# Weights packed slot by slot, and their low parts made by a negative on ScalarE and an accumulating DMA

## The chip, the cores and the metric

The kernel runs on one core of a Trainium2 chip. The metric is the time of one execution on the device in microseconds (us); lower is better. The core has the engines TensorE (PE; its weight loads are shown apart as PEld), VectorE (DVE), ScalarE (ACT), GpSimd (POOL) and SyncE (SP, which issues transfers), and 16 DMA engines that all queues share.

## The reference

Two blocks run on 512 tokens of width 1024, all in float32. Block one has two layers; each normalizes, multiplies by `w_in`, forms five attention branches, and merges them through gates and `w_branch`:

```
h = _rmsnorm(x, norm_g)
p = _split_columns(h @ w_in)
... five branches y_a (dsa), y_b (fox), y_c (sb), y_d (nsa), y_e (mem) ...
merge = sigmoid(p['merge'])
merged = sum(merge * einsum('bsnc,ncd->bsnd', ys, w_branch), axis=2)
return x + merged @ w_out
```

Block two adds 256 context tokens. Its first part, called the conformer part here, is a projection with `ab_w_in`, a 31-tap convolution over time of 512 channels beside an mLSTM with four heads, and a projection with `ab_w_out`. An FFN (ffn0), an attention with low-rank projections (MLA) and a second FFN (ffn1) follow.

## The kernel before

Every large matrix is multiplied in split precision. A float32 weight W is split into hi = W rounded to the type fp32r and lo = W − hi; activations are split alike, and `mm3` makes each product out of three matmuls, hi·hi, hi·lo and lo·hi.

Weights come in **slots** of at most 128 partitions by 1024 elements (512 KB). A slot is `m` row tiles of 128 rows by `n` columns with m·n ≤ 1024, for instance eight row tiles by 128 columns of `w_in`. For a slot, `wtile` does three things:

- a DMA that SP issues fills `wraw` straight out of the matrix in DRAM; each partition gets m pieces of n elements (eight of 512 bytes for the slot just named);
- ACT copies `wraw` to `whi` (L119 `CAST whi<-wraw`, `nc.scalar.copy`), which rounds it;
- DVE or POOL computes `wlo` = `wraw` − `whi` (`tt`, L741 `TENSOR_TENSOR wlo<-wraw,whi`).

There are four buffers each of `wraw`, `whi` and `wlo`, so a slot can be prepared once the slot four before it has been used up. In all 461 slots pass.

Nothing runs in the order in which the code is written. The class `Plan` records every operation (which is why nearly all instructions have line L119, that of the recorder), and at each `flush` a list scheduler sorts a part's operations into an order for each engine, going by a table of durations. Operations recorded with `either` may go to one of several engines: `tt` to DVE or POOL, `ev` (evictions and copies) to DVE or ACT. Which one is the planner's choice, so a change of what an engine has to do also moves other work. Once the order is made it is fixed: an engine runs its instructions one after the other and waits where one isn't ready.

Three places in the program are spoken of later:

- **Block one, the merges** (`zm`): for each branch and each of eight column tiles d, a `w_in` slot gives 24 matmuls into `ps_mm`, ACT makes the gate (`ACTIVATE gt<-ps_mm`, a tanh), and six matmuls into `ps_br` use a `w_branch` slot, which is held for four values of d. Then comes `w_out`.
- **The conformer part:** DVE computes the convolution, 31 operations for each of four channel tiles (`SCALAR_TENSOR_TENSOR u<-apad,cw,u`, 128x783); beside it PE does the heads of the mLSTM, whose matrices `dm` DVE also multiplies. The `ab_w_out` slots (tile names `wlo`, `whi` like all) are prepared meanwhile.
- **The start:** `w_mem_kv` is loaded and split while the first normalizations run.

Of the kernel before, what the change touches and what calls it, by code (L numbers as in the profile page):

```python
# [19 lines left out]
P = 128  # L20
# [71 lines left out]


class Op:
    __slots__ = ("i", "prio", "alts", "left", "ready", "succ", "tiles", "first", "table", "nbytes", "best", "end", "vis", "done", "nm", "why", "cols", "preds", "port", "kind")


class PlannedPool:
# [34 lines left out]
class Plan:  # L133
# [55 lines left out]
    def cost(self, eng, name, outs, ins, a, k):  # L189
        n = max(self.size(x) for x in outs[:1] + [y for y in ins if name in ("tensor_reduce", "max")])  # L190
        if eng == "t":
            cols = self.size(outs[0])
            big = ins[0].dtype in (F32, F32R)
            if name == "transpose":
                return max(2 * cols / 2.4, 107.0) + 2.5 if big else 56.0
            if ins[0].dtype == F32:
                if outs[0].ap[0][1] == 32:
                    return cols / 2.4 + 8
                if outs[0].ap[0][1] == 64:
                    return max(2 * cols / 2.4, 107.0) + 11  # L200
                return 2 * max(2 * cols / 2.4, 107.0) + 5
            if ins[0].dtype == F32R:
                return max(cols / 2.255, 107.0) + 2.5
            return max(cols / 2.4, 53.0) + 2.5
        src_psum = any(self.in_psum(x) for x in ins)
        if eng == "s":
            c = n * 0.8333 + (51 if src_psum else 93)
            if len([x for x in ins if self.size(x) == 1]) and n > 1:
                c += 94
            return c + (92 if k.get("accum_out") is not None else 0)  # L210
        if eng == "v":
            if name == "memset":
                return n * 1.04 + 8
            if name == "reciprocal":
                return n * 8.33 + 65
            if name == "tensor_tensor_scan":
                return n * 2.08 + 65
            two = name in ("tensor_copy", "tensor_scalar", "scale") and not src_psum and not self.in_psum(outs[0])
            ptr = name in ("tensor_scalar", "scalar_tensor_tensor", "scale") and n > 1 and any(self.size(x) == 1 for x in ins)
            return n * (0.52 if two else 1.0417) + (129 if ptr else 67)  # L220
        if eng == "g":
            if name == "memset":
                return n * 0.9 + 30
            return n * (2.1 if name in ("tensor_tensor", "scale") else 4.2) + 150
        return 600.0
# [8 lines left out]
    def add(self, alts, name, a, k):  # L234
        outs = [a[0]]
        if k.get("accum_out") is not None:
            outs.append(k["accum_out"])
        ins = [x for x in a[1:] if _is_ap(x)] + [x for kk, x in k.items() if kk != "accum_out" and _is_ap(x)]
        op = Op()
        op.i = len(self.ops)  # L240
        op.prio = op.i
        op.alts = [(e, fn, self.cost(e, name, outs, ins, a, k)) for e, fn in alts]
        op.cols = 0.0
        if alts[0][0] == "t":
            dt = ins[0].dtype
            big = name != "transpose" and dt == F32
            op.cols = (4 if big else 1) * self.size(outs[0]) * ins[0].ap[0][1] / P
        op.port = self.shares(name, outs, ins)
        op.kind = None
        if alts[0][0] == "t":  # L250
            up = lambda x: 32 if x <= 32 else 64 if x <= 64 else 128
            op.kind = (name == "transpose", ins[0].dtype, up(ins[0].ap[0][1]), up(outs[0].ap[0][1]))
        op.left, op.ready, op.succ, op.done = 0, 0.0, [], False
        op.table = None
        if name == "activation":
            func = a[2] if len(a) > 2 else k.get("func")
            op.table = TABLES.get(str(func).split(".")[-1])
        op.nm, op.why = name + ":" + a[0].tensor.name.rsplit("_", 1)[0], None
        if name == "matmul" and ins[0].dtype == F32:
            op.nm += "*"  # L260
        op.nbytes = 4 * self.size(outs[0]) * outs[0].ap[0][1] if alts[0][0] == "y" else 0
        preds = set()
        tiles = []
        for ap, wr in [(x, False) for x in ins] + [(x, True) for x in outs]:
            nm = ap.tensor.name
            if nm in self.tile_of and nm not in tiles:
                tiles.append(nm)
            r = self.region(ap)
            W, R = self.hist.setdefault(nm, ([], []))
            hit = lambda q: q[0] < r[1] and r[0] < q[1] and q[2] < r[3] and r[2] < q[3]  # L270
            inside = lambda q: r[0] <= q[0] and q[1] <= r[1] and r[2] <= q[2] and q[3] <= r[3]
            mem = self.tile_of.get(nm)
            serial = wr and alts[0][0] == "t" and mem is not None and mem[2] == PSUM
            for q, o in W:
                if hit(q) or (serial and (o.alts if o.done else o.alts[0][0]) == "t"):
                    preds.add(o)
            if wr:
                for q, o in R:
                    if hit(q):
                        preds.add(o)  # L280
                W[:] = [(q, o) for q, o in W if not inside(q) or o is op]
                R[:] = [(q, o) for q, o in R if not inside(q)]
                W.append((r, op))
            else:
                R.append((r, op))
        if alts[0][0] == "t":
            tiles += [x.tensor.name for x in self.into if x.tensor.name not in tiles]
        preds.discard(op)
        op.preds = list(preds) if DEBUG else ()
        for p in preds:  # L290
            if p.done:
                at = p.end if len(op.alts) == 1 and p.alts == op.alts[0][0] != "y" else p.vis
                op.ready = max(op.ready, at)
            else:
                p.succ.append(op)
                op.left += 1
        op.tiles = tiles
        self.ops.append(op)
# [86 lines left out]
    def flush(self):  # L385
# [97 lines left out]
        while remaining:  # L483
# [114 lines left out]
                GAPS[kk] = GAPS.get(kk, 0) + t - free[e]  # L598
            free[e] = end
            vis = end + self.LAT[e]  # L600
            if e == "y":
                dma_free = max(t + 1300, dma_free) + o.nbytes / 350.0
                vis = dma_free + 300
            o.end, o.vis = end, vis
            order.append((t, len(order), fn))
            if DEBUG:
# [31 lines left out]
                        parked[tag] = []  # L638
            for q in o.succ:
                q.left -= 1  # L640
                at = end + self.SAME[e] if len(q.alts) == 1 and q.alts[0][0] == e and e != "y" else vis
                if q.alts[0][0] == "t" and e != "t":
                    at += self.TO_PE
                if at > q.ready:
                    q.ready, q.why = at, o.nm
                if q.left == 0:
                    push(q)
# [46 lines left out]
class Net:  # L694
    def __init__(self, ctx, tc, I):
        ctx.enter_context(tc.manual_schedule())
        self.plan = self.nc = Plan(tc)
        self.tc, self.I, self.ctx = tc, I, ctx
        self.ahead = {}
        self.cst = self.plan.pool(ctx, "cst")  # L700
        self.wp = self.plan.pool(ctx, "wp")
        self.mm = self.plan.pool(ctx, "mm", PSUM)
        self.dr = ctx.enter_context(tc.tile_pool(name="dr", bufs=1, space=bass.MemoryType.DRAM))
# [60 lines left out]
    def wraw(self, src, m, n):  # L764
# [2 lines left out]
        self.nc.sync.dma_start(rv, src.rearrange("(k p) n -> p k n", p=P))  # L767
        return rv

    def prefetch(self, src, n, count, keep=True):  # L770

        K = src.shape[0]
# [10 lines left out]

    @staticmethod
    def key(src, m, n):
        return src.tensor.name, src.offset, m, n

    def wtile(self, src, m, n):
        if self.key(src, m, n) in self.ahead:
            return self.ahead.pop(self.key(src, m, n))  # L790
        rv = self.wraw(src, m, n)
        hi = self.wp.tile([P, 1024], F32R, tag="whi", name="whi", bufs=4)
        lo = self.wp.tile([P, 1024], F32R, tag="wlo", name="wlo", bufs=4)
        hv = hi[:, :m * n].rearrange("p (k n) -> p k n", n=n)
        lv = lo[:, :m * n].rearrange("p (k n) -> p k n", n=n)
        self.nc.scalar.copy(hv, rv)
        self.tt(lv, rv, hv.bitcast(F32), ALU.subtract, m * n)
        return hv, lv

    def mm3(self, ps, a, b, start, stop):  # L800
# [940 lines left out]
class BlockTwo:  # L1741
# [485 lines left out]
    def ffn(self, l, h, xT, xc, beside=None, after=None):  # L2227
# [5 lines left out]
        with ExitStack() as c2:  # L2233
            wk = n.plan.pool(c2, f"ffn{l}")
            n.wk, n.nt2 = wk, 6
            first = len(n.plan.ops)
            w = I["ffn_w_in_2"][l]
            starts = [1, S + 2]
# [252 lines left out]
def body(tc, I, out):  # L2491
    with ExitStack() as ctx:
        net = Net(ctx, tc, I)
        nc = net.nc
        net.consts(net_off())
        xp = net.plan.pool(ctx, "xp")
# [5 lines left out]
        for d in range(KD):  # L2502
            nc.sync.dma_start(out[d * P:(d + 1) * P, :], xT[:, d])
        net.plan.flush()


def net_off():
    return const_arrays()[1]


_INS = ["positions", "norm_g", "w_in", "kv_norm", "w_uk", "w_uv", "fox_bias", "nsa_pe_k", "nsa_pe_v",
        "nsa_wc1_k", "nsa_wc2_k", "nsa_wc1_v", "nsa_wc2_v", "mem_norm", "w_mem_kv", "w_branch", "w_out", "final_norm",
# [29 lines left out]
```

## Time and profile before

| | |
|---|---|
| time, median of 3 runs (us) | 3224.23 (3220.99 to 3225.24) |
| the profiled execution (us) | 3226.99, its span 3224.5 |
| mean granted TensorE clock in it | 0.975 of full speed |
| PE busy | 94% |
| DVE busy | 71% |
| ACT busy | 43% |
| POOL busy | 6% |
| moved by DMA | 287.9 MB, 89 GB/s over the span |

The profile is of one execution; busy time of an engine leaves out waits and the issuing of DMAs. In the rows further down PE's share is that of matmuls whose ends are modelled, so that idle time between matmuls is read better than the duration of one. In time, block one takes about 0 to 1500 us, the conformer part 1500 to 1890, ffn0 to 2440, MLA to 2860, and ffn1 the rest.

### The profile page before, as it was taken

Reading aid. Unit: us, or ns where it says so; the run is one execution under the profiler, and the core shown is the slowest. Engines: PE = TensorE matmul, PEld = TensorE weight load, DVE = VectorE, ACT = ScalarE, POOL = GpSimd, SP = SyncE. Lnnn points to the kernel's source line nnn. Section 1 sums busy time; section 2 is a strip of 40 time slices with the busy share of each in tenths; the row PEclk is TensorE's granted clock in tenths of the full one; section 3 lists DMA queues with packets and bytes.
Section 4 is the critical chain, followed back from the end, with each engine's and each line's share of the span. In section 5 each row is a group of like instructions: output and inputs, shape, how many; then the busy total and the mean of one; then the engine's idle time right before and its main releaser. Section 6 shows DMA issues by size and latency. Waiting matters only on the chain.

```text
span 3224.5 us, 43815 instructions
## 1 busy us (share of the span) xinstructions
PE 3042.2 (94%) x16384; PEld 2506.6 (78%) x16392; DVE 2300.3 (71%) x4600; ACT 1379.4 (43%) x2840; POOL 202.4 (6%) x197
## 2 busy tenths in 40 slices
PE   6899898999899898998997999999999999989999
PEld 5678776787778687787976888888887777768887
DVE  8795878756896778756899677655547878765555
ACT  5544545424445445424325632222225766642332
POOL 1100000001100000001222010000000001110000
PEclk9899999999999899999998999999999999999999
DMA  6343142444342142443310124334322100023323
GB/s 172 94 111 97 46 128 76 118 128 126 104 115 80 49 127 69 121 124 102 101 59 27 47 79 125 106 109 139 106 60 74 30 10 28 27 76 108 105 78 93
DMA packets 383597, 287.90 MB, mean 89 GB/s; under 512 B 13324, under 2 KB 352536, under 8 KB 383128
## 3 DMA queue, kind: packets, MB, share of 16 engines
q1 hardware_dynamic: 383384, 285.10, 30.6%
q8 instruction: 129, 2.11, 0.3%
q14 instruction: 84, 0.69, 0.1%
HBM read 269.72 MB, written 8.52 MB: 86 GB/s over the span
## 4 chain that ended last, share of the span: by engine, by line
PE 47%; DVE 11%; ACT 3%; DMA 3%; issue 2%; SPq 0%; POOL 0%; DVEq 0%; ACTq 0%; POOLq 0%
PE ps_mm L119 39%; DVE u L119 3%; DMA wraw<-in_ada_wT_dram 2%; PE ps_tp L119 2%; PE ps_pv L119 2%; PE ps_lg L119 2%; PE ps_br L119 1%; PE ps_nd L119 1%; DVE mx L119 1%; ACT p L119 1%; DVE y_mod L119 1%; DVE wlo L741 1%; PE ps_st L119 1%; DVE ada_junk L119 1%; DVE sq L119 0%
## 5 line engine op out<-in xcount | busy, mean ns | idle before, releaser
L119 ACT CAST whi<-wraw 128x1024 fp32r<-128x1024 f32 (+8 forms) x461 | 409.3, 889 | 817.9 <-PE ps_mm L119 749.7
L119 PE MATMUL ps_mm<-h_ffn,whi 128*128 128x512 f32 (+1 forms) x2112 | 565.0, 356 | 7.4 <-ACT h_ffn L119 5.5
L741 DVE TENSOR_TENSOR wlo<-wraw,whi 128x1024 fp32r<-128x1024 f32 (+5 forms) x389 | 402.0, 1034 | 134.3 <-ACT whi L119 129.6
L119 PEld LDWEIGHTS ps_mm<-h_ffn,whi 128*128 128x128 f32 x2112 | 375.5, 190 | 68.2 <-ACT h_ffn L119 7.9
L119 PE MATMUL ps_mm<-hh,whi 128*128 128x512 f32 x960 | 389.5, 406 | 3.4 <-ACT whi L119 3.4
L119 PE MATMUL ps_mm<-hl,whi 128*128 128x512 f32 x960 | 388.9, 405 | 0.0
L119 PE MATMUL ps_mm<-hh,wlo 128*128 128x512 f32 x960 | 387.7, 404 | 0.0
L119 PE MATMUL ps_mm<-h_ffn,wlo 128*128 128x512 f32 (+1 forms) x1056 | 374.3, 355 | 0.0
L119 DVE CUSTOM_DVE_ANT_0 ada_junk<-wraw,cond,cols 128x1024 bf16<-128x1024 f32 x160 | 209.2, 1308 | 107.5 <-DMA wraw<-in_ada_wT_dram 106.2
L741 POOL TENSOR_TENSOR wlo<-wraw,whi 128x1024 fp32r<-128x1024 f32 (+4 forms) x72 | 152.9, 2128 | 1389.5 <-ACT whi L119 811.5
L119 PEld LDWEIGHTS ps_mm<-h_ffn,wlo 128*128 128x128 f32 x1056 | 200.1, 190 | 27.6
L119 PEld LDWEIGHTS ps_mm<-hh,whi 128*128 128x128 f32 x960 | 182.8, 190 | 38.3 <-ACT whi L119 4.6
L119 PEld LDWEIGHTS ps_mm<-hh,wlo 128*128 128x128 f32 x960 | 182.5, 190 | 35.1 <-DVE wlo L741 1.0
L119 ACT ACTIVATE p<-ps_lg,mx 128x384 f32<-128x384 f32 (+3 forms) x288 | 155.8, 544 | 122.9 <-DVE mx L119 119.0
L119 PEld LDWEIGHTS ps_mm<-hl,whi 128*128 128x128 f32 x960 | 182.8, 190 | 33.0
L119 PE MATMUL ps_mm<-fhi,whi 128*128 128x512 f32 (+1 forms) x528 | 187.6, 356 | 2.6 <-DVE xT L119 2.6
L119 PE MATMUL ps_mm<-flo,whi 128*128 128x512 f32 (+1 forms) x528 | 188.3, 357 | 0.0
L119 PE MATMUL ps_mm<-fhi,wlo 128*128 128x512 f32 (+1 forms) x528 | 187.6, 355 | 0.0
L119 DVE SCALAR_TENSOR_TENSOR xT<-ps_mm,mod,xT 128x512 f32<-128x512 f32 x136 | 101.7, 749 | 88.5 <-PE ps_mm L119 88.0
L119 DVE TENSOR_REDUCE mx<-ps_lg 128x1 f32<-128x384 f32 (+3 forms) x288 | 143.8, 505 | 25.9 <-PE ps_lg L119 22.5
L119 PE MATMUL ps_tp<-ident,p 128*128 128x128 f32 x768 | 131.9, 282 | 18.2 <-DVE p L736 8.3
L119 PEld LDWEIGHTS ps_tp<-ident,p 128*128 128x128 f32 x768 | 91.4, 142 | 62.7 <-ACT p L737 20.1
(533 smaller groups left out, 6314.6 us busy)
## 6 DMA issues: line engine op xcount, KB each, us to landing
wraw<-in_w_in_dram SPq DMA_DIRECT2D x132, 512.0 KB
wraw<-in_ada_wT_dram SPq DMA_DIRECT2D x96, 512.0 KB
wraw<-in_ffn_w_in_dram SPq DMA_DIRECT2D x88, 512.0 KB
wraw<-in_ffn_w_out_dram SPq DMA_DIRECT2D x64, 256.0 KB
wraw<-in_w_branch_dram SPq DMA_DIRECT2D x20, 512.0 KB
wraw<-in_w_out_dram SPq DMA_DIRECT2D x16, 512.0 KB
wraw<-in_ab_w_in_dram SPq DMA_DIRECT2D x16, 512.0 KB
wraw<-in_ffn_w_out_dram SPq DMA_DIRECT2D x32, 192.0 KB
```

What stands on the lines that cost most here:

```text
L119: return plan.add([(eng, lambda: fn(*a, **k))], name, a, k)
L741: f = lambda x: x.tensor_tensor(out, a, b, op=op)
```

## The change

Two things change.

**Packing.** The host lays out all slots, in the order in which the program asks for them, in one array `in_w_dram` of 461 x 128 x 1024 elements. A slot is then one block in which each partition's elements lie together (4 KB for a full slot), and SP loads it with one DMA as before.

**Low parts.** While `lo_by_dma` is set, which is through block one and the conformer part, `wlo` is not a subtraction any more. ACT writes the negated and rounded weights into `wlo` (`activation`, Copy with scale −1), and a DMA issued by POOL reads the slot from DRAM a second time and adds it to `wlo` (`accum_op=ALU.add`). The first call of `ffn` clears the flag; from there on DVE or POOL subtracts as before. 230 slots are made in the new way: 187 subtractions leave DVE and 43 leave POOL, 230 activations come to ACT, and 230 DMAs to POOL's queue. The number of SP's DMAs doesn't change. The planner gets a cost for a DMA on POOL and its landing, and moves some 60 evictions from ACT to DVE (`pT`, `yh`, `sb_v`, `p` and others).

```diff
@@ cost
         if eng == "g":
+            if name == "dma_start":
+                return 1000.0
@@ flush
-            if e == "y":
+            if o.dma:
                 dma_free = max(t + 1300, dma_free) + o.nbytes / 350.0
-                vis = dma_free + 300
+                vis = dma_free + (300 if e == "y" else 1500)
@@ class Net
+    lo_by_dma = True
+
+    def packed(self, src, m, n):
+
+        self.packs.append((src, m, n))
+        return self.I["w"][len(self.packs) - 1][:, :m * n]
+
+    def wpacked(self, src, m, n):
+        raw = self.wp.tile([P, 1024], F32, tag="wraw", name="wraw", bufs=4)
+        dr = self.packed(src, m, n)
+        self.nc.sync.dma_start(raw[:, :m * n], dr)
+        return raw[:, :m * n].rearrange("p (k n) -> p k n", n=n), dr
...
     def wtile(self, src, m, n):
...
-        rv = self.wraw(src, m, n)
+        rv, dr = self.wpacked(src, m, n)
...
         self.nc.scalar.copy(hv, rv)
-        self.tt(lv, rv, hv.bitcast(F32), ALU.subtract, m * n)
+        if self.lo_by_dma:
+
+            self.nc.scalar.activation(lv, rv, AF.Copy, scale=-1.0)
+            self.nc.gpsimd.dma_start(lo[:, :m * n], dr, accum_op=ALU.add)
+        else:
+            self.tt(lv, rv, hv.bitcast(F32), ALU.subtract, m * n)
         return hv, lv
@@ ffn
             n.wk, n.nt2 = wk, 6
+            n.lo_by_dma = False
@@ kernel
+    for slot, (src, m, n) in zip(w, packs, strict=True):
+        slot[:, :m * n] = src.reshape(m, P, n).transpose(1, 0, 2).reshape(P, m * n)
```

What it does to the order on the engines is seen at three places. The first is ACT in the merge of the last branch (dsa) of layer 0, before; `gt` is the gate, `mh` the merged result that goes on to `w_out`:

```order
L119 ACTIVATE gt<-ps_mm 128x512
L119 CAST whi<-wraw 128x1024
L119 ACTIVATE gt<-ps_mm 128x512
L119 CAST whi<-wraw 128x1024 x2
L119 ACTIVATE gt<-ps_mm 128x512
L119 CAST whi<-wraw 128x1024
L119 ACTIVATE gt<-ps_mm 128x512
```

And now, on the same engine at the same place:

```order
L119 CAST whi<-wraw 128x1024
L119 ACTIVATE gt<-ps_mm 128x512
L119 ACTIVATE wlo<-wraw 128x1024
L119 CAST whi<-wraw 128x1024
L119 ACTIVATE gt<-ps_mm 128x512
L119 ACTIVATE wlo<-wraw 128x1024
L119 CAST whi<-wraw 128x1024
L119 ACTIVATE wlo<-wraw 128x1024
L119 CAST whi<-wraw 128x1024
L119 ACTIVATE gt<-ps_mm 128x512
```

A slot's negative stands behind its cast and, mostly, behind a gate that waits for PE. The second place is POOL in the conformer part; `b` and `M` are matrices of the mLSTM, `u<-u,mu` the layer norm behind the convolution, `gpad` the first instruction of ffn0. Before:

```order
L741 TENSOR_TENSOR wlo<-wraw,whi 128x1024
L119 MEMSET apad 128x15 x6
L741 TENSOR_TENSOR wlo<-wraw,whi 128x1024 x4
L119 MEMSET b 64x768
L119 MEMSET M 64x768
L741 TENSOR_TENSOR wlo<-wraw,whi 128x1024 x12
L741 TENSOR_TENSOR u<-u,mu 128x512 x4
L741 TENSOR_TENSOR u<-u,mu 128x256 x3
L119 MEMSET gpad 128x1 x9
```

And now:

```order
L119 DMA wlo<-in_w_dram 128x792 x2
L119 DMA wlo<-in_w_dram 128x528
L119 DMA wlo<-in_w_dram 128x1024 x2
L119 MEMSET b 64x768
L119 DMA wlo<-in_w_dram 128x1024 x2
L119 MEMSET M 64x768
L119 DMA wlo<-in_w_dram 128x1024 x12
L744 TENSOR_TENSOR u<-u,mu 128x512 x4
L119 DMA wlo<-in_w_dram 128x1024 x8
L119 MEMSET gpad 128x1 x9
```

POOL has no subtraction left there, and the last eight slots of `ab_w_out`, which were DVE's, now stand on POOL behind the layer norm. The third place is DVE at the last channel tile of the convolution, whose taps stand between the products `dm` of the heads. Before:

```order
L119 TENSOR_SCALAR u<-apad,cw,cols 128x783
L119 SCALAR_TENSOR_TENSOR u<-apad,cw,u 128x783 x20
L119 TENSOR_TENSOR dm<-ps_mb,u 128x128
L119 SCALAR_TENSOR_TENSOR u<-apad,cw,u 128x783
L119 TENSOR_TENSOR dm<-ps_mb,u 128x128
```

And now:

```order
L119 TENSOR_SCALAR u<-apad,cw,cols 128x783
L119 SCALAR_TENSOR_TENSOR u<-apad,cw,u 128x783 x31
L728 COPY mv<-ps_mm 128x4x128
L119 SCALAR_TENSOR_TENSOR u<-apad,cw,u 128x783
L119 TENSOR_TENSOR dm<-ps_mb,u 128x128
L119 SCALAR_TENSOR_TENSOR u<-apad,cw,u 128x783
L119 TENSOR_TENSOR dm<-ps_mb,u 128x128
```

More of the taps now stand ahead of the first `dm`.

## Rows read from the trace of the kernel before

**Rows 1.** The page's first part: busy time, share of the span, instructions.

```profile
span 3224.5 us, 43815 instructions
PE 3042.2 (94%) x16384; PEld 2506.6 (78%) x16392; DVE 2300.3 (71%) x4600; ACT 1379.4 (43%) x2840; POOL 202.4 (6%) x197
```

**Rows 2.** Busy time by stretch: PE, PEld, DVE, ACT, POOL; clock; DMA share; GB/s.

```profile
0.00:1500.00 1500.00, 1384.33 (x7146) 1126.92 (x7155) 1131.99 (x2422) 692.22 (x1343) 84.94 (x76) 0.97 0.37 105
1640.00:1760.00 120.00, 100.83 (x513) 82.54 (x511) 110.69 (x165) 38.99 (x108) 32.69 (x15) 0.89 0.15 44
```

**Rows 3.** Chain that ended last, 1590 to 1840 us: start, us, what.

```profile
1647.59 31.06 DVE u L119 x27
1682.34 20.45 DVE u L119 x22
```

**Rows 4.** Six stretches of block one, sums; all work, then the subtractions.

```profile
sum 220.00, PE 195.04 PEld 157.79 DVE 208.64 ACT 127.23 POOL 23.33; mean PE 32.51 PEld 26.30 DVE 34.77 ACT 21.21 POOL 3.89
...
sum 220.00, PE 77.02 PEld 41.40 DVE 14.34 POOL 17.84; mean PE 12.84 PEld 6.90 DVE 2.39 POOL 2.97
```

**Rows 5.** Waits of PE, 0 to 1890 us: total, times, longest; then of PEld.

```profile
PE ps_z L119 <- DVE sb_later L741: 11.8, 9, 2.4
...
PEld ps_mm L119 <- DVE wlo L741: 1.0, 2, 0.8
```

**Rows 6.** Lines by form, 0 to 1890 us: busy, mean ns | idle before, releasers.

```profile
L119 ACT CAST whi<-wraw 128x1024 fp32r<-128x1024 f32 x204 | 213.7, 1049 | 351.7 <-PE ps_mm L119 295.0 <-issue 38.8 <-DMA wraw<-in_w_in_dram 8.1
L741 DVE TENSOR_TENSOR wlo<-wraw,whi 128x1024 fp32r<-128x1024 f32 x168 | 205.0, 1221 | 117.5 <-ACT whi L119 116.7
...
L119 DVE SCALAR_TENSOR_TENSOR u<-apad,cw,u 128x783 f32<-128x783 f32 x120 | 138.1, 1188 | 0.6
...
L741 POOL TENSOR_TENSOR wlo<-wraw,whi 128x1024 fp32r<-128x1024 f32 x36 | 100.4, 2794 | 651.3 <-ACT whi L119 651.3
```

**Rows 7.** The subtractions alone by stretch: PE, PEld, DVE, POOL, clock, DMA share, GB/s.

```profile
0.00:1500.00 1500.00, 636.66 (x1690) 326.35 (x1691) 206.81 (x173) 62.67 (x26) 0.97 0.37 105
1640.00:1760.00 120.00, 34.97 (x95) 18.17 (x94) 0.00 (x0) 25.84 (x8) 0.89 0.15 44
```

**Rows 8.** Timeline of POOL and DVE, 1696 to 1722 us: start, us, instruction.

```profile
1701.94 12.23 POOL L741 TENSOR_TENSOR wlo<-wraw,whi 128x1024 fp32r<-128x1024 f32 x4 [34.59 <-ACT whi L119]
...
1702.90 2.97 DVE L119 SCALAR_TENSOR_TENSOR u<-apad,cw,u 128x783 f32<-128x783 f32 x1
...
1715.12 1.02 DVE L119 SCALAR_TENSOR_TENSOR u<-apad,cw,u 128x783 f32<-128x783 f32 x1
```

**Rows 9.** The taps: durations in ns, min/median/max, first and last start.

```profile
L119 DVE SCALAR_TENSOR_TENSOR u<-apad,cw,u x120: 1018/1026/3171, 1557.4 to 1733.1; 128x783 f32<-128x783 f32 x120
```

**Rows 10.** Timeline of ACT in a merge, 1400 to 1445 us: start, us, instruction, idle before.

```profile
1414.53 1.05 ACT L119 CAST whi<-wraw 128x1024 fp32r<-128x1024 f32 x1 [5.42 <-PE ps_mm L119]
1415.49 0.58 ACT L119 ACTIVATE gt<-ps_mm 128x512 f32<-128x512 f32 x1
```

**Rows 11.** Chain in ffn0, 1990 to 2300 us: DMAs from issue to landing.

```profile
2072.09 3.46 DMA wraw<-in_ada_wT_dram
...
2077.61 5.02 DMA wraw<-in_ada_wT_dram
```

**Rows 12.** Chain in that merge, 1384 to 1440 us: start, us, what.

```profile
1414.73 1.37 PE ps_br L119 x6
1416.10 5.59 PE ps_mm L119 x24
...
1430.04 5.59 PE ps_mm L119 x24
```

**Rows 13.** Two short stretches, columns as in group 2.

```profile
640.00:720.00 80.00, 80.00 (x352) 64.63 (x353) 49.85 (x71) 23.55 (x32) 0.00 (x0) 1.00 0.45 129
20.00:30.00 10.00, 2.60 (x9) 1.59 (x9) 7.41 (x14) 8.83 (x17) 0.00 (x0) 1.00 1.02 285
```

**Rows 14.** GB/s at the start, 0 to 30 us in slices of 0.75.

```profile
GB/s 0 0 90 88 322 153 350 415 295 235 376 412 358 411 415 381 124 4 6 100 276 337 320 294 267 320 357 345 342 306 296 290 292 290 309 333 198 315 347 19
```

More of the change, by code (lines that the diff above doesn't have):

```diff
@@ L94 @@
 class Op:
-    __slots__ = ("i", "prio", "alts", "left", "ready", "succ", "tiles", "first", "table", "nbytes", "best", "end", "vis", "done", "nm", "why", "cols", "preds", "port", "kind")
+    __slots__ = ("i", "prio", "alts", "left", "ready", "succ", "tiles", "first", "table", "nbytes", "best", "end", "vis", "done", "nm", "why", "cols", "preds", "port", "kind", "dma")
 class PlannedPool:
@@ L260, in add @@
             op.nm += "*"
-        op.nbytes = 4 * self.size(outs[0]) * outs[0].ap[0][1] if alts[0][0] == "y" else 0
+        op.dma = name == "dma_start"
+        op.nbytes = 4 * self.size(outs[0]) * outs[0].ap[0][1] if op.dma else 0
         preds = set()
@@ L291, in add @@
             if p.done:
-                at = p.end if len(op.alts) == 1 and p.alts == op.alts[0][0] != "y" else p.vis
+                at = p.end if len(op.alts) == 1 and p.alts == op.alts[0][0] and not p.dma else p.vis
                 op.ready = max(op.ready, at)
@@ L640, in flush @@
                 q.left -= 1
-                at = end + self.SAME[e] if len(q.alts) == 1 and q.alts[0][0] == e and e != "y" else vis
+                at = end + self.SAME[e] if len(q.alts) == 1 and q.alts[0][0] == e and not o.dma else vis
                 if q.alts[0][0] == "t" and e != "t":
@@ L698, in __init__ @@
         self.tc, self.I, self.ctx = tc, I, ctx
-        self.ahead = {}
+        self.ahead, self.packs = {}, []
         self.cst = self.plan.pool(ctx, "cst")
@@ L785, in key @@
     def key(src, m, n):
-        return src.tensor.name, src.offset, m, n
+        return src.__array_interface__["data"][0], m, n
     def wtile(self, src, m, n):
@@ L2493, in body @@
         net = Net(ctx, tc, I)
+        packs = net.packs
         nc = net.nc
@@ L2504, in body @@
         net.plan.flush()
+    return packs
 def net_off():
     return const_arrays()[1]
+_STREAMED = ("w_in", "w_mem_kv", "w_branch", "w_out", "ab_w_in_2", "ab_w_out_2", "mla_w_in_2", "mla_w_uq_2", "mla_w_ukv_2",
+             "mla_w_out_2", "ffn_w_in_2", "ffn_w_out_2")
+SLOTS = 461
 _INS = ["positions", "norm_g", "w_in", "kv_norm", "w_uk", "w_uv", "fox_bias", "nsa_pe_k", "nsa_pe_v",
@@ L2532 @@
             name, a = "ada_wT_2", np.ascontiguousarray(a.transpose(0, 2, 1))
-        put(name, a)
+        if name in _STREAMED:
+            I[name] = a
+        else:
+            put(name, a)
     for name, src in (("xT", "x"), ("memT", "mem"), ("ctxT", "ctx_2")):
@@ L2536 @@
     put("consts", const_arrays()[0])
+    I["w"] = nc.dram_tensor("in_w_dram", (SLOTS, P, 1024), F32, kind="ExternalInput").ap()
     out = nc.dram_tensor("out_0_dram", (D, S), F32, kind="ExternalOutput").ap()
     with tile.TileContext(nc) as tc:
-        body(tc, I, out)
+        packs = body(tc, I, out)
+    w = np.zeros((SLOTS, P, 1024), np.float32)
+    for slot, (src, m, n) in zip(w, packs, strict=True):
+        slot[:, :m * n] = src.reshape(m, P, n).transpose(1, 0, 2).reshape(P, m * n)
+    arrays["in_w_dram"] = w
     r = bass_utils.run_bass_kernel_spmd(nc, [arrays], core_ids=[0])
```

## The prediction

> **What bounds the kernel now.** I read the page's totals first, then busy time by stretch, the groups of instructions by form, the waits of PE, the chain of work that ended last, and timelines of single stretches. PE is busy for 3042 of 3224.5 us and DVE for 71% [rows 1]: TensorE is the bound nearly everywhere, and no matmul is taken away here. Something is to be had only where PE stands idle or runs at a lower clock, and where DVE is what it waits for. Block one leaves PE idle for 1500 − 1384.3 = 115.7 us; in the middle of the conformer part PE is busy for 100.8 of 120 us at a clock of 0.89 while DVE is busy for 110.7 [rows 2]. There the chain runs through the convolution's taps, 31.1 and 20.5 us at a stretch [rows 3]. In block one DVE sets the pace in short pieces: in six stretches of 220 us together, which I chose because DVE is nearly full in them (208.6 us), PE is idle for 25.0 us [rows 4]; a typical single wait there is that for `sb_later`, 11.8 us in nine pieces [rows 5]. For low parts themselves PE waits almost never: 1.0 us for those of DVE in all of this [rows 5].
>
> **What is removed.** A subtraction of a full slot takes 1.221 us on DVE and 2.794 on POOL [rows 6]. Of those of DVE 168 are full ones, 205 us, nearly all in block one, where DVE spends 206.8 us on all its subtractions and POOL 62.7 [rows 7].
>
> The conformer part first. POOL makes eight low parts between 1640 and 1760 us, 25.8 us, and DVE none [rows 7]; still DVE is slowed by them. Four of them in a row on POOL take 12.2 us from 1701.9 on, and the taps that start meanwhile take 2.97 us; as soon as POOL is done a tap takes 1.02 [rows 8]. The median of the 120 taps is 1.026 us, their mean 1.188, so that 120 x 0.162 = 19.4 us of DVE go to such meetings [rows 6, 9]. With a DMA on POOL in place of the subtraction they should end. How much of it reaches the end of the part? At least these four taps' delay, 4 x (2.97 − 1.02) = 7.8. At most all of PE's loss in that stretch, 19.2 us idle and 0.11 x 100.8 = 11.1 of clock [rows 2]: 30. The taps lead the chain for most of the stretch, so I take nearly the whole relief: **−18 us** (−30 to −7.8). What is late next are the heads' own products and `ab_w_out`, whose slots now queue on POOL behind the layer norm; that queue was idle for hundreds of us before its subtractions [rows 6], and I give it nothing.
>
> In block one the relief of DVE is larger, some 200 us, and the share that lies on the path smaller. In the six stretches the subtractions cost DVE 14.3 us, and POOL's 17.8 us beside them hold up what DVE does then, if it acts as in the conformer part [rows 4]. The idle time of PE there, 25.0 us, is the most to be had; the least is nothing, since about 60 evictions come from ACT to DVE and the planner can spend the gap on them. I take less than DVE's own 14.3: **−10 us** (−25 to 0).
>
> **What is added.** *ACT.* 230 negatives of the size of the cast, 1.049 us for a full slot [rows 6]: at most 241 us, fewer for small slots. ACT is busy for 692 of 1500 us in block one [rows 2]; with nearly all of these it comes to about 930, or 62%, less what it passes to DVE. In the six stretches it is at 127 of 220. It is covered by PE's matmuls, since ACT waits for PE for 295 us ahead of casts alone [rows 6]; in the sum 0. Without that cover a negative costs PE 1.05 us each time.
>
> *The way to a low part.* Before: cast, then 1.2 us of DVE. Now: cast (1.05), mostly a gate (0.58, [rows 10]), the negative (1.05), POOL's issue, and a DMA that has to land. An accumulating DMA is nowhere in the trace. An ordinary load of 512 KB takes 3.46 to 5.02 us from issue to landing where the chain waits for it [rows 11]; below I take that, above twice the longer one, 10 us. So the way is 6.1 to 12.7 us. What is there for it: in a merge a d takes 5.59 + 1.37 = 6.96 us [rows 12], and a slot cast at 1414.5 is used at 1430.0, a lead of 15.5 us [rows 10, 12]. That is enough at either end. It is not where two `w_branch` slots are held at once, of four buffers, so that the `w_in` slots rotate through two: the lead is then about 6.96 + 1.37 = 8.3 us. There are 2 layers x 5 branches x 2 = 20 such places. At the lower end nothing is late; at 10 us of landing 4.4 us are, of which a change of the order by the planner saves some: I set the upper bound at 2 us a place, +40. I choose a landing near that of the ordinary load, since as much data is read, and add a little for the places where it is longer: **+3 us** (0 to +40). Only POOL's other work queues behind a DMA that waits there, and that is 84.9 us in block one, most of it subtractions [rows 2, 7].
>
> [...]
>
> *The DMA engines.* They move 105 GB/s in block one at a share of 0.37 [rows 2]. The load is densest between 640 and 720 us, 129 GB/s at 0.45 [rows 13], that is 10.3 MB, about 20 slots. At the start 512 KB go at up to 415 GB/s where pieces are long (`xT`, 4 KB a row) and near 300 where they are 512 bytes (the slices from the 24th on) [rows 14]: 1.3 against 1.7 us. Packed, 20 loads take 26 us of these 80; 14 accumulating DMAs (DVE made 14 low parts there) take 18 us if they go like a load, 37 if at half its rate. It is full only if one costs more than three loads, 26 + 55 = 81. In the sum 0.
>
> *Packing* itself shortens a load by 0.4 us, but casts wait for raw data for only 8.1 us in 1890 [rows 6]: 0. Where the new low parts aren't used the order of work is nearly as before: 0.
>
> *The start.* From 20 to 30 us the DMA engines are full (1.02), PE does 2.6 us [rows 13], and `w_mem_kv` is being loaded; each of its low parts now needs a second DMA. For the first four slots I count 4 x 1.3 = 5 us more against 4 x 0.4 less: **+4 us** (0 to +12).
>
> **Sum.** −18 − 10 + 3 + 4 = −21 against the 3227.0 us of the profiled execution, whose 2.5 us outside the span [rows 1] don't change: 3206. That execution lies 2.8 us above the median of 3224.2, so for the median I say **3203 us**, 0.7% faster. About 0.2%, 6.4 us, is what a measurement of this kernel can tell from no change.
>
> **Rivals.** *Low parts land late* (slower). If an accumulating DMA lands after more than 8.3 − 2.7 = 5.6 us, all 20 places wait; at two us each the sum is −18 − 10 + 40 + 4 = +16, 3240, and with the 4.4 us of the upper end each, +88, nearer to 3290. For it: the chain of five steps through three queues and half the slots' lead. Against it: everywhere else there are 15.5 us. It decides for slower from some 31 us of waits on, 1.5 us a place.
>
> *ACT takes DVE's place* (no change). ACT sits in the path of the gates and of `p`; if its negatives, which can stand ahead of an eviction, cost PE as much as DVE gives back, a tenth of the 230 on the path is 24 us: 3224. For it, ACT at 58% in the six stretches already; against it, evictions that move to DVE.
>
> [...] If POOL's part in an accumulating DMA holds DVE up as its subtractions do, the taps stay long: −10 + 7 = −3, 3221, and with the DMAs stretched by DVE in turn some us more. Rows show only that the two engines get in each other's way [rows 8], not by which kind of work. [...]
>
> **How the numbers follow.** Forecast 0.52, low parts late 0.25, ACT 0.12, the lock 0.11. The forecast's own range is 3172 (both gains at their upper end) to 3217. Towards no change and slower it meets the two middle rivals; the late rival up to about 3255 holds most of its 0.25. So **3165 to 3255**. Faster: 0.52, and a third of the two middle cases, 0.59; same 0.14; slower 0.27.
>
> **What the profile of after would show.** Right: a tap's mean near 1.03 us and none of 2.9; PE's share between 1640 and 1760 over 90%, its clock nearer 1; DVE in block one some 150 us less, ACT some 200 more; PE's waits for `wlo` of a few us. Wrong: waits of PE on a DMA into `wlo`, 20 of them a few us long, behind changes of `w_branch`; new idle time on gates; a DMA share near 1 beyond the start; or taps as long as before.

## The result and the profile after

The change makes the kernel slower: 3258.0 us (3257.6 to 3259.0) against 3224.2, a ratio of 1.0105 (95% interval 1.0092 to 1.0117). The forecast was 3203, in a range from 3165 to 3255.

First the page of the changed kernel, its totals, and the queues that it lists (packets, MB, share of the time of all 16 DMA engines) with the line of the new DMAs (count, KB each, median us from issue to landing):

```profile
span 3256.1 us, 44294 instructions
PE 3050.6 (94%) x16384; PEld 2513.7 (77%) x16392; DVE 2083.1 (64%) x4480; ACT 1551.7 (48%) x3004; POOL 282.9 (9%) x379
...
q1 hardware_dynamic: 107544, 285.10, 27.1%
q0 software_dynamic: 33120, 116.90, 19.9%
...
wlo<-in_w_dram POOLq DMA_DIRECT2D x204, 512.0 KB, 7.9
```

DVE lost 217 us of work and ACT gained 172 [rows 1]. But a low part lands 7.9 us after its DMA is issued, and the 230 of them take 0.199 x 3256.1 / 230 = 2.82 us each of all DMA engines on the mean (204 of them are full slots).

To see where the time went, the kernels are cut at four marks that all have: the first matmul of the form `ps_mm<-hh,whi` (layer 0 begins in earnest), the first `ps_mm<-mh,whi` (`w_out` of layer 0), the last `ps_mm<-mh,wlo` (end of block one), and the first `ps_mm<-h_ffn,whi` (ffn0). They stand in the view of a tile's instructions, here of the changed kernel (min/median/max ns, first and last start):

```profile
L119 PE MATMUL ps_mm<-hh,whi x960: 386/394/793, 81.7 to 1514.9; 128*128 128x512 f32 x192
...
L119 PE MATMUL ps_mm<-mh,whi x128: 389/393/505, 765.2 to 1561.6; 128*128 128x512 f32 x128
L119 PE MATMUL ps_mm<-mh,wlo x128: 389/393/504, 766.0 to 1562.0; 128*128 128x512 f32 x128
...
L119 PE MATMUL ps_mm<-h_ffn,whi x2112: 274/389/794, 1926.5 to 3234.5; 128*128 128x512 f32 x127, 128*128 128x256 f32 x65
```

The lengths between the marks, worked out in this way for the profiled execution of each kernel (us; times are medians, and profiled executions lie up to 7 us from them, so that a few us between two rows say little). The profiled execution of e11 was a slow one of 9710 us; e16 repeats that kernel.

| kernel | start | layer 0 | layer 1 | conformer | rest | time |
|---|---|---|---|---|---|---|
| before | 77.8 | 655.9 | 769.9 | 387.3 | 1333.6 | 3224 |
| after | 81.7 | 683.5 | 796.8 | 364.5 | 1329.6 | 3258 |
| e1 packing alone | 75.7 | 656.4 | 766.9 | 388.7 | 1329.6 | 3217 |
| e2 conformer alone | 75.2 | 654.3 | 769.8 | 369.6 | 1327.5 | 3193 |
| e3 eight rows | 73.4 | 657.0 | 767.3 | 362.1 | 1328.9 | 3189 |
| e4 plain copy | 74.3 | 655.8 | 774.4 | 361.7 | 1331.0 | 3201 |
| e5 no negative | 77.5 | 654.6 | 759.1 | 359.2 | 1333.3 | 3184 |
| e6 POOL reads | 75.8 | 655.8 | 764.4 | 407.0 | 1329.7 | 3235 |
| e7 planner told | 80.7 | 679.9 | 800.2 | 361.4 | 1329.3 | 3252 |
| e8 MLA too | 75.2 | 652.1 | 769.1 | 366.4 | 1341.7 | 3211 |
| e9 late, light | 90.2 | 699.3 | 813.3 | 371.2 | 1330.8 | 3306 |
| e10 load, early | 80.8 | 661.4 | 787.8 | 363.0 | 1329.5 | 3232 |
| e12 e2, planner told | 75.6 | 654.4 | 768.9 | 364.1 | 1327.8 | 3191 |
| e13 e3, POOL free | 73.8 | 659.0 | 765.5 | 363.8 | 1328.0 | 3193 |
| e14 e9, POOL free | 90.3 | 676.2 | 791.1 | 363.9 | 1328.1 | 3245 |
| e15 after, POOL free | 82.5 | 678.7 | 803.6 | 365.0 | 1326.8 | 3261 |
| e16 half on POOL | 75.4 | 651.6 | 769.0 | 382.6 | 1330.1 | 3212 |

The start got 4 us longer, each layer of block one 27, the conformer part 23 shorter. The two layers, by busy time in the stretches between the marks, the first one from 3 us behind its mark on (PE, PEld, DVE, ACT, POOL, clock, DMA share, GB/s), before:

```profile
81.00:733.70 652.70, 612.44 (x3164) 496.79 (x3169) 494.64 (x1091) 301.94 (x595) 29.28 (x29) 0.97 0.36 100
733.70:1503.40 769.70, 724.79 (x3672) 587.44 (x3676) 572.18 (x1182) 346.79 (x666) 44.90 (x34) 0.97 0.36 101
```

and after:

```profile
85.00:765.20 680.20, 622.57 (x3163) 503.41 (x3167) 428.79 (x1043) 360.77 (x648) 79.85 (x102) 0.95 0.64 158
765.20:1562.00 796.80, 733.98 (x3672) 593.32 (x3675) 475.40 (x1121) 424.39 (x741) 97.60 (x121) 0.95 0.68 164
```

PE is idle for 57.6 and 62.8 us in place of 40.3 and 44.9, 35 us more, and the same matmuls take 10.1 and 9.2 us more at a mean granted clock of 0.95 in place of 0.97. Together that is the 54.6 us by which the two stretches grew. DVE has 163 us less to do and gives nothing for it; the DMA share goes from 0.36 to 0.66. PE's largest wait in the whole span is a new one (us in total, times, longest):

```profile
PE ps_mm L119 <- DMA wlo<-in_w_dram: 32.7, 14, 4.8
PE ps_tp L119 <- ACT p L740: 18.6, 16, 6.1
```

Of these 14 waits 11, 22.1 us in all, lie in the two layers, two, 6.8 us together, in the start, and one of 3.8 in the conformer part. Two of the places, in the chain of work that ended last (start, us, what). One is in the last merge of layer 0:

```profile
724.36 1.38 PE ps_br L119 x6
725.74 2.25 PE ps_mm L119 x10
727.99 6.08 issue
734.07 0.01 POOLq L119
734.08 8.90 DMA wlo<-in_w_dram
742.98 0.14 issue
743.12 6.90 PE ps_mm L119 x22
```

Here two `w_branch` slots are held: ACT casts the slot at 731.2, its low part is issued at 734.1 and lands at 743.0, 11.8 us after the cast, and PE stands for 3.0 us. In the other the raw weights themselves have only just come, and the way to the low part stands behind them in full:

```profile
422.67 3.63 DMA wraw<-in_w_dram
426.32 1.04 ACT whi L119
427.37 0.97 ACT wlo L119
428.35 0.28 ACT hid_s L728
428.73 9.43 DMA wlo<-in_w_dram
```

In all, thirteen such DMAs stand on the chain, 4 to 10 us each. The conformer part answers to what was shown before: the taps there (rows of groups 6 and 9) now all take the same time, also the 26 that run while POOL issues a DMA.

```profile
L119 DVE SCALAR_TENSOR_TENSOR u<-apad,cw,u x120: 1019/1034/1039, 1615.7 to 1762.4; 128x783 f32<-128x783 f32 x120
```

### The profile page after: what moved, and what is told of

It is laid out like the page before. It is cut to its first block, busy times and chain, and to the rows that moved or that the text cites. A ratio compares the mean times of both kernels' runs of the same rounds, so it can differ in the third digit from the quotient of the medians.

```text
span 3256.1 us, 44294 instructions
## 1 busy us (share of the span) xinstructions
PE 3050.6 (94%) x16384; PEld 2513.7 (77%) x16392; DVE 2083.1 (64%) x4480; ACT 1551.7 (48%) x3004; POOL 282.9 (9%) x379
## 4 chain that ended last, share of the span: by engine, by line
PE 65%; DVE 15%; DMA 7%; issue 7%; ACT 6%; POOL 0%; SPq 0%; ACTq 0%; DVEq 0%; POOLq 0%
PE ps_mm L119 51%; DMA wlo<-in_w_dram 3%; DMA wraw<-in_ada_wT_dram 3%; PE ps_tp L119 3%; PE ps_pv L119 3%; PE ps_lg L119 2%; PE ps_br L119 2%; DVE score L119 1%; DVE m L119 1%; PE ps_nd L119 1%; DVE mx L119 1%; DVE ada_junk L119 1%; PE ps_st L119 1%; ACT p L119 1%; PE ps_z L119 1%
## 5 line engine op out<-in xcount | busy, mean ns | idle before, releaser
L119 PE MATMUL ps_mm<-hh,wlo 128*128 128x512 f32 x960 | 394.7, 411 | 22.1 <-DMA wlo<-in_w_dram 22.1
L119 POOL DMA_DIRECT2D wlo<-in_w_dram x230 | 200.4, 871 | 1457.4 <-ACT wlo L119 1167.3
L119 ACT ACTIVATE wlo<-wraw 128x1024 fp32r<-128x1024 f32 (+4 forms) x230 | 236.3, 1027 | 11.1 <-PE ps_mm L119 11.0
L744 DVE TENSOR_TENSOR wlo<-wraw,whi 128x1024 fp32r<-128x1024 f32 (+5 forms) x202 | 179.1, 888 | 11.4 <-ACT whi L119 8.1
```

Source lines behind the costliest of these rows:

```text
L119: return plan.add([(eng, lambda: fn(*a, **k))], name, a, k)
L744: f = lambda x: x.tensor_tensor(out, a, b, op=op)
```

## The experiments

All times are medians, compared with the kernel before on the same chip; it took 3223.5 to 3224.6 us on each, so that runs of different chips are compared with each other too.

**e1, packing alone.** The flag is off from the beginning; the order of work is that of before.

```diff
-    lo_by_dma = True
+    lo_by_dma = False
```

> Packing alone: all low parts by subtraction, in the order of work of the kernel before. Both theories (low parts that land late; ACT's new work) put the whole loss on the low parts, so 3224 us within 4. If the packed array itself costs, by transfers that come at other times, 3230 or more; if it is a gain by itself, 3215 or less.

3216.9 us, ratio 0.9976 (0.9967 to 0.9986): a small gain of its own, 7 us, 4 of them behind the conformer part. The loss is that of the low parts.

**e2, the conformer part alone.**

```diff
-    lo_by_dma = True
+    lo_by_dma = False
...
         xT = one.run(xp)
+        net.lo_by_dma = True
         xT, _ = two.run(xp, xT)
```

> Negative and accumulating DMA in the conformer part alone, block one subtracts. If the loss is all of block one and the conformer's gain stands by itself: 3224 - 23 = 3201 us, within 5. If the gain in the conformer part was only what block one had left over (idle PE, work done ahead), 3218 to 3226.

3193.0 us, ratio 0.9897 (0.9880 to 0.9913). The conformer part is 19 us shorter than e1's, and nothing is lost elsewhere: the gain stands by itself.

**e3, accumulating on eight partitions.** The planner's figure for the size is kept (its line is left out here), so that all orders stay those of after.

```diff
...
-            self.nc.gpsimd.dma_start(lo[:, :m * n], dr, accum_op=ALU.add)
+            self.nc.gpsimd.dma_start(lo[:8, :m * n], dr[:8], accum_op=ALU.add)
```

> The same order on every engine, but each accumulating DMA adds only 8 of the 128 partitions (32 KB in place of 512); the low parts of the other 120 stay the negated weights. Landing theory: low parts land in about 3 us in place of 7.9, PE's waits for them vanish, block one ends where it did before or some 10 us sooner, and the time is 3185 to 3200 us. ACT theory: negatives and moved evictions stay, so the time stays above 3245.

3189.3 us, ratio 0.9889 (0.9874 to 0.9903): 69 us less than after, with every instruction of PE, DVE, ACT and POOL in the same order. The low parts land in 3.7 us:

```profile
q0 software_dynamic: 7360, 7.33, 1.4%
...
wlo<-in_w_dram POOLq DMA_DIRECT2D x204, 32.0 KB, 3.7
```

The loss is therefore in the DMA's landing or load, not in ACT's new work or in POOL's issuing, which stay (230 issues of 0.79 us in place of 0.87). But the layers are at 657.0 and 767.3 us, where e1, with all subtractions, has 656.4 and 766.9: even with low parts in time, block one gains nothing from DVE's relief.

**e4, a plain copy.** The same 512 KB are read, and nothing is added.

```diff
-            self.nc.gpsimd.dma_start(lo[:, :m * n], dr, accum_op=ALU.add)
+            self.nc.gpsimd.dma_start(lo[:, :m * n], dr.bitcast(F32R))
```

> The same order and the same bytes read, but POOL's DMA copies the slot into the low part in place of adding to it, so that the low part is the weight itself. If the accumulation's second source is what makes the landing long, landing falls from 7.9 to some 5 us and half of the loss or more goes: 3205 to 3235 us. If it is the issue by POOL and the extra bytes, landing stays over 7 and the time over 3245. ACT theory: over 3245 with a short landing.

3201.4 us, ratio 0.9928 (0.9913 to 0.9943). Landing and load fall together, to 0.108 x 3197.2 / 230 = 1.50 us of the engines a slot:

```profile
q0 software_dynamic: 33120, 116.90, 10.8%
...
wlo<-in_w_dram POOLq DMA_DIRECT2D x204, 512.0 KB, 5.1
```

By this comparison the bytes read a second time cost 12 of the 69 us, and the adding 57.

**e5, e4 without the negative.**

```diff
-            self.nc.scalar.activation(lv, rv, AF.Copy, scale=-1.0)
-            self.nc.gpsimd.dma_start(lo[:, :m * n], dr, accum_op=ALU.add)
+            self.nc.gpsimd.dma_start(lo[:, :m * n], dr.bitcast(F32R))
```

> As e4 (a plain copy into the low part, which is then the weight itself), and without the negative on ACT. Why did block one gain nothing in e3 and e4, though the subtractions were gone and the low parts in time? If ACT's 236 us of negatives and the evictions behind them took the place, block one gets 15 to 40 us shorter than e4's and the time is 3165 to 3185 us. If DVE's subtractions were never on the path there, block one stays within 8 us of e4's and the time is 3195 to 3202.

3184.3 us, ratio 0.9877 (0.9861 to 0.9893): 17 us under e4; in the profiled executions layer 1 is 15 us shorter. ACT's work costs something there. Part of it can be the shorter way, since a low part no longer stands behind its negative, and the planner moved evictions; this isn't taken apart.

**e6, POOL's reading put back.** As e2; behind each DMA of the conformer part POOL subtracts the slot once more, in pieces of 128 columns into a tile that nobody reads.

```diff
             self.nc.gpsimd.dma_start(lo[:, :m * n], dr, accum_op=ALU.add)
+            for c in range(0, m * n, 128):
...
+                self.nc.gpsimd.tensor_tensor(junk[:, :e - c], raw_[:, c:e], hi[:, c:e].bitcast(F32), op=ALU.subtract)
```

> As e2 (conformer part alone), and behind each DMA in the conformer part POOL reads the slot and its rounded copy again, in pieces of 128 columns whose results nobody uses: POOL's old work is back, DVE has no subtraction. If the gain there came from DVE no longer meeting POOL's subtractions, taps grow to 2 us and more beside them and the conformer part goes from 370 back to 383 us or more, 3205 to 3220 in all. If it came from DVE's own subtractions or the new order, it stays below 375 and the time within 5 us of 3193.

3234.5 us, ratio 1.0037 (1.0022 to 1.0052). More than any theory said, and not for the reason that was to be tested: in small pieces POOL needed 181 us between 1496 and 1903 us, and they took 20% of the chain there. The taps are longer (median 1.112 us, the longest 1.504), but the length of the part tells nothing on them; e11 takes its place.

**e7, the planner told the landing.**

```diff
-                dma_free = max(t + 1300, dma_free) + o.nbytes / 350.0
-                vis = dma_free + (300 if e == "y" else 1500)
+                dma_free = max(t + 1300, dma_free) + o.nbytes / (350.0 if e == "y" else 180.0)
+                vis = dma_free + (300 if e == "y" else 3700)
```

> The whole change, with the planner told what the trace shows of an accumulating DMA (180 GB/s and 3.7 us behind its data, about 7.9 us from issue to landing). If the order of work could hide the landing, had the planner known it, 3225 to 3240 us. If leads are bound by the four buffers and the DMA engines, within 8 us of 3258.

3251.9 us, ratio 1.0087 (1.0071 to 1.0103): 6 us less than after, and the two intervals overlap. PE's direct wait for low parts falls from 22.1 us in the form below to 4.9 (idle before it, after the second bar), but the layers stay at 680 and 800:

```profile
L119 PE MATMUL ps_mm<-hh,wlo 128*128 128x512 f32 x960 | 389.5, 407 | 4.9 <-DMA wlo<-in_w_dram 4.9
```

PE is idle for 119.5 us of the two layers, after for 120.4. An order that waits less for low parts waits elsewhere; for what, and which part of it is the load, was not taken apart.

**e8, MLA too.** As e2, with the flag set again at the beginning of `mla`.

> As e2, and the low parts of the MLA part by negative and DMA as well. POOL makes 25 subtractions there (28.5 us) beside DVE, at 321 of 420 us. If their meeting costs there what it did in the conformer part, the MLA part gets 5 to 12 us shorter: 3181 to 3188 us. If landing costs it as in block one, or ACT, busy for 269 of 420 us, has no room, 3195 to 3215.

3210.6 us, ratio 0.9957 (0.9941 to 0.9973), 18 above e2; the part behind the conformer is 14 us longer, with 10.3 us of waits for low parts between 2430 and 2860 us. POOL's and DVE's meetings aren't worth that there.

**e9, late but light.** In the order of after, each low part gets two accumulating DMAs of 8 partitions, the second behind the landing of the first.

```diff
...
-            self.nc.gpsimd.dma_start(lo[:, :m * n], dr, accum_op=ALU.add)
+            add = lambda g, r: g.dma_start(lo[r, :m * n], dr[r], accum_op=ALU.add)
+            self.plan.either("dma_start", {"g": lambda g: (add(g, slice(0, 8)), add(g, slice(0, 8)))[1]}, lo[:8, :m * n], dr[:8])
```

> The order of after, and each low part gets two accumulating DMAs of 8 partitions (32 KB each), the second behind the landing of the first: about 3.7 + 3.7 us, as late as after's 7.9, with hardly any load on the DMA engines. (120 of 128 partitions of the low parts stay negated weights.) If lateness alone makes the loss, block one is 40 us or more longer than e3's and the time 3230 to 3265 us. If it is the time that the accumulation takes of the DMA engines, within 10 us of e3's 3189.

3306.0 us, ratio 1.0255 (1.0235 to 1.0274). Lateness costs a lot, but PE also waits 40 us for `roped`, `cmp_e` and `sb_later`, which POOL makes, and POOL's queue stands still until the first DMA of a pair has landed (559 us in all up to 1620). So this run doesn't show lateness alone; e14 takes its place.

**e10, loaded but early.** As e3, then two copies into a scratch array that nobody reads.

```diff
...
+            self.plan.either("dma_start", {"g": lambda g: (add(g, slice(0, 8)), g.dma_start(s0[:, :m * n], dr),
+                                                           g.dma_start(s1[:, :m * n], dr[:96]))[0]}, lo[:8, :m * n], dr[:8])
```

> The order of after, an accumulating DMA of 8 partitions for each low part as in e3, and behind it two copies from DRAM to DRAM, of 1.75 slots together, whose results nobody reads. They are to take some 2.6 us of all DMA engines a slot, as after's accumulation does (2.8). If the load on the DMA engines makes the loss, by raw weights and other transfers that come late, 3225 to 3265 us. If lateness of the low parts alone makes it, within 12 us of e3's 3189.

3231.7 us, ratio 1.0024 (1.0013 to 1.0036), 42 above e3. The load was as meant, 0.185 x 3222.5 / 230 = 2.59 us a slot:

```profile
q0 software_dynamic: 24160, 211.91, 18.5%
...
wlo<-in_w_dram POOLq DMA_DIRECT2D x204, 32.0 KB, 4.4
```

Load costs, in layer 1 above all (787.8), and makes the small DMAs later too, 4.4 in place of 3.7 us. PE has no wait for low parts in the two layers here. What comes late are ordinary transfers, which DVE waits for in the two layers: slots of `ada_wT`, the weights of a small product that DVE makes on the side, and `x_old`, the input of a layer that is added at its end. In e3 (no wait for `x_old`) and in e10:

```profile
DVE ada_junk L119 <- DMA wraw<-in_ada_wT_dram: 28.2, 13, 3.2
```

```profile
DVE ada_junk L119 <- DMA wraw<-in_ada_wT_dram: 59.3, 19, 8.3
DVE xT L119 <- DMA x_old<-in_xT_dram: 20.7, 5, 11.2
DVE xT L119 <- DMA x_old<-x_keep: 10.8, 2, 10.5
```

In after they are 59.1, 14.7 and 10.6 us. How much of this reaches PE was not measured.

**e11 and e16, half of the low parts back on POOL.** As e2; in the conformer part POOL subtracts every second slot.

```diff
-        if self.lo_by_dma:
+        if self.lo_by_dma and len(self.packs) % 2:
+            self.nc.gpsimd.tensor_tensor(lv, rv, hv.bitcast(F32), op=ALU.subtract)
+        elif self.lo_by_dma:
```

> As e2, but in the conformer part POOL subtracts every second slot's low part, some 14, as it did before; DVE still subtracts none. If DVE's meetings with POOL's subtractions were what the conformer part lost, taps of 2 to 3 us are back, their mean rises by 0.15 us or more, and the part goes from 370 to 380 us or more; 3203 to 3215 in all. If DVE's own subtractions or the order were the cause, it stays below 374 and the time within 5 us of 3193.

3213.0 us, ratio 0.9966 (0.9954 to 0.9977), 20 above e2. For a profile of this kernel, e16:

> e11 again, for its profile: 3213 us within 3; by the meeting of POOL and DVE a tap's mean of 1.18 us or more with single ones over 2 us, and a conformer part of 380 us or more; without it 1.03 and 370.

3212.5 us, ratio 0.9964 (0.9951 to 0.9977). The part is 382.6 us long, 13 more than e2's, and long taps are back (last line: e2's taps):

```profile
L119 DVE SCALAR_TENSOR_TENSOR u<-apad,cw,u x120: 1018/1026/3117, 1549.8 to 1717.8; 128x783 f32<-128x783 f32 x120
...
L119 DVE SCALAR_TENSOR_TENSOR u<-apad,cw,u 128x783 f32<-128x783 f32 x120 | 129.3, 1117 | 0.6
...
L119 POOL TENSOR_TENSOR wlo<-wraw,whi 128x1024 fp32r<-128x1024 f32 x14 | 51.4, 3673 | 165.9 <-ACT whi L119 162.6 <-PE ps_mm L119 3.4
...
L119 DVE SCALAR_TENSOR_TENSOR u<-apad,cw,u 128x783 f32<-128x783 f32 x120 | 121.6, 1030 | 2.3
```

The mean tap is 1.117 us against 1.030 in e2, less than expected, but 120 x 0.087 = 10.4 us of the 13 are seen in the taps alone. Six taps take over 1.5 us, and each of them runs beside a subtraction of POOL's, as do all ten such taps of the kernel before. DVE subtracts nothing in either run, so this is the meeting and not DVE's own work. The two runs also differ in their order, to which the other 3 us can belong.

**e12, e2 with the planner told** (the edits of e2 and e7).

> e2, with the planner told the landing that the trace shows, as in e7. Where leads are long (the conformer part keeps PE busy with 15 us a slot and more) an order that starts low parts sooner can save the few waits left: 3186 to 3192 us. If it costs nothing now, within 3 us of 3193.

3191.5 us, ratio 0.9904 (0.9889 to 0.9919). No different from e2 by these intervals. Both beat before and after.

**e13, e14, e15: e3, e9 and the whole change with POOL free.** Up to the first FFN POOL gets no element-wise work by choice and no memset:

```diff
+        if self.nopool and "v" in engines:
+            engines = {e: f for e, f in engines.items() if e != "g"}
...
```

> e3 (DMAs of 8 partitions), with POOL given nothing but the DMAs up to the first FFN; its other work goes to DVE. The yardstick for e14 and e15: within 10 us of e3's 3189.

> e9 (two DMAs of 8 partitions, one behind the other, some 7 us in all) with POOL given nothing but DMAs. If lateness is the larger part, 40 us or more above e13. If the load is, less than 25 above e13.

> The whole change with POOL given nothing but the DMAs: late and loaded. Lateness theory: within 15 us of e14. Load theory: 40 us or more above e14. Both alike: some 65 above e13, with e14 in the middle.

3192.6, 3244.5 and 3261.2 us (ratios 0.9906, 0.9891 to 0.9921; 1.0067, 1.0052 to 1.0082; 1.0122, 1.0105 to 1.0138). The orders of PE, DVE and ACT are the same in all three. Lateness costs 52 us over e13; the load on top of it 17 more. In e14 the DMAs go one behind the other, at 3.2% of the engines:

```profile
q0 software_dynamic: 14720, 14.67, 3.2%
...
wlo<-in_w_dram POOLq DMA_DIRECT2D x408, 32.0 KB, 3.3
...
PE ps_mm L121 <- DMA wlo<-in_w_dram: 37.9, 16, 6.3
```

From the end of the negative to the landing a low part of the two layers takes 7.8 us in e14 and 8.3 in e15 (medians; 4.1 in e13), so that e14 is as late as the change. In the start it is later, 11.9 us against 8.9, since POOL waits for each first DMA: the start is 90.3 us long, 82.5 in e15. In the two layers alone lateness costs 43 us, and both together 58.

## Why the prediction was wrong

*The conformer part: right.* −18 was forecast; e2 gives −19 against e1, the whole change −23. The mechanism is the one that was named, DVE's taps held up by POOL's subtractions: without them all taps take 1.03 us, with half of them the long taps and 13 us are back (e16). In the kernel before all ten taps over 1.5 us (2.57 to 3.17 us) stand beside subtractions of POOL; the 26 taps that in after stand beside POOL's DMA issues take 1.024 to 1.039 us. So the rival that has 0.11, by which POOL's part in the new DMAs holds DVE up as its subtractions do, did not come true, and that DVE in turn delays the issues no run shows either: in after all 230 take 0.85 to 1.02 us. Why the part is 5 to 8 us shorter still in after and e3 than in e2 was not tried.

*The way to a low part: the step that failed.* "I choose a landing near that of the ordinary load, since as much data is read", +3 us. The landing is 7.9 us, past the 5.6 from which by the first rival all 20 places wait, and its 3240 to 3290 hold the 3258. That number is in part luck: the rival has 20 waits behind changes of `w_branch`, 40 us or more, and the two layers have 11 waits of 22 us in all; it also keeps the −10 that didn't come and gives the load nothing. The bytes were no measure of it: a copy of the same bytes lands in 5.1 us and costs 12 (e4), the adding makes the rest. Lateness is worth 52 us (e14, of which the start has more than the change gives it), load with low parts only 0.7 us later 42 (e10), both 69 (e3 to after, e13 to e15), so that they overlap. The prediction also priced a place at its wait. In the trace PE's waits for low parts are 22 of the 55 us that the two layers lost, 19 are matmuls at the lower clock, and e7 shows that the time lost doesn't go away with these waits. Nor are the places only the 20 in the merges: at 428 us a slot has no lead at all, because its raw weights had just come.

*The load on the DMA engines: 0 was forecast.* "It is full only if one costs more than three loads" was asked of a whole stretch of 80 us; an accumulation costs 2.82 us, 1.9 times the plain copy's 1.50, and a mean share of 0.63 to 0.64 in the two layers went with a loss of 42 us in e10: transfers come late without the engines being full. The prediction's upper case, half a load's rate, was an assumption that no row or run shows; its 37 us for 14, 2.6 us each, come near the 2.82 measured. Why an accumulation takes longer than a copy was not tested.

*Block one's gain: wrong too.* −10 was forecast for DVE's relief. With low parts in time it is 0 (e3 and e1 differ by 0.6 and 0.4 us in the two layers). That a full DVE and an idle PE stand side by side in six stretches didn't show that subtractions were what PE waited for; PE's waits there had been for other things [rows 5]. ACT's negatives, which the sum had at 0, can have taken it: in e5, where neither DVE nor ACT makes the low part, the two layers are 1413.7 us long, 10 shorter than e1's 1423.3. As e5's order and its way to a low part differ too, this isn't shown.

*The range.* The forecast's own range ends at 3217, which is 3224.2 − 7.8 with no cost added. By the bounds that stand in the prediction, −7.8, 0, +40 and +12, the same sum goes up to 3268, past the 3255 that was given.

*Small terms.* The start: +4 forecast, +4 measured (−2 by packing, e1, and +6 by the low parts). Packing: 0 forecast, −7 measured (e1), 4 of them behind the conformer part.

## What to carry to other kernels

A transfer that takes the place of an element-wise instruction is priced by its landing and by what it takes of the DMA engines, and both are to be measured for just that kind of transfer; an accumulating one is neither a load nor a copy (here 7.9 us to landing and 2.82 us of the engines, against a copy's 5.1 and 1.50). Ask for how long the result of each step can be late with the buffers there are, at the place with the shortest lead, before counting what the relieved engine saves. Where a step pays in one part of a program (here the conformer part, 31 us with the packing) and costs in another, apply it there alone.

## What was not expected of the hardware

An accumulating DMA of 512 KB from DRAM, issued by POOL, takes 7.9 us from issue to landing (after), a plain one 5.1 (e4); 32 KB still take 3.7 (e3). On the mean of all 230 it takes 2.82 us of all 16 engines, a plain one 1.50. It also keeps POOL longer, 0.87 us against 0.54 in e4 (means of 230):

```profile
L119 POOL DMA_DIRECT2D wlo<-in_w_dram x230 | 200.4, 871 | 1457.4 <-ACT wlo L119 1167.3
```
